# Pointwise convolution of a hybrid encoder block: from four plain column-block products to two groups of two blocks with seven-product pairs

## The chip, the cores and the metric

One Trainium2 chip, one of its cores. The metric is the device time of one execution in microseconds (us), the median of several runs. The program before takes 2043.55 us (three runs: 2043.1, 2043.55, 2046.21).

## The reference, cut to what matters

One layer of an encoder block works on x of 256 rows (two halves of 128) and 4096 columns. A projection by `w_in` gives q, k, v and z_a for a chunked attention, and a, g and z_c for a convolution module. The end of that module is what the change touches:

```python
u = jax.nn.silu(layer_norm(u, ln_g, ln_b))       # (256, 2048)
y_c = u @ w_pw + b_pw                            # w_pw: (2048, 2048)
y_c = rms_norm(y_c, conv_out_g) * jax.nn.silu(z_c)
h = h + concat([y_a, y_c]) @ w_out               # then a gated embedding, then a final norm
```

`u @ w_pw + b_pw` is the pointwise convolution: 256 rows by 2048 columns, a sum over 2048.

## The kernel before

**How a product is made.** Every fp32 operand is split into a high part (rounded to fp32r) and a low part (the rest), and a product is three matmuls: high by high, low by high, high by low. A matmul takes 128 of the sum's columns (a k-block), one half h of the rows, and 512 columns of the weight. For each weight tile `wt` of 128x1024 (512 KB, five buffers) ScalarE casts the high part `wh` (L203) and VectorE subtracts it to get the low part `wl` (L204); `wh` and `wl` have three buffers each, so the casts of a tile wait until TensorE has done with the tile three before it.

**Plain products.** `product` (L223) does one block of 512 columns in two of the four accumulator banks of PSUM, twelve matmuls for each weight tile.

**Seven-product pairs.** `mixed_product` (L324) does two column blocks j at once over both row halves h, in all four accumulator banks `c[h][j]`. Its k-blocks go in pairs, in an order written out as text; a pair is plain (eight products of three matmuls, 24) or, with a star, done by seven products (21 matmuls) in the manner of Strassen and Winograd. A starred pair needs more of the other engines: the two weight tiles are added up in four ways (`ua`, `ub`: L423, L424, L427, L428, VectorE, 128x512 each), and `ua` and `ub` are split like weights (`uh`, `ul`, two buffers each); three of the weight quarters are split as such, and one isn't. On the operand's side four sums of its quarters are needed, the combinations: `combine_again` (L275) rebuilds the quarters (L279, 128x512), forms four sums (L256 to L259, 128x128 each) and splits them (L264 ScalarE, L265 VectorE). Four of the seven products go into helper banks P1, P5, P6, P7, which are all four banks of the pool that the attention uses for its scores and transposes. After the last starred pair `on_helpers` runs: `helper_sums` (L461) adds the helpers up, four additions on VectorE that read PSUM. The end adds each accumulator to its sum, once for each quarter (h, j).

**The stage.** The attention's last heads come first (L829 to L858), then the pointwise convolution (L914 to L921): for each of four column blocks c a row of the bias is loaded and spread over the partitions, a plain `product` of 16 k-blocks runs on the operand `uS`, and VectorE adds the bias while reading PSUM (L919), and ScalarE takes the sum of squares (L497). Then come the combinations of all of x, `xS` (L926 to L930, eight times `combine_again`), and the products for z_a (`gated`, L932), two column blocks at a time by `mixed_product` in the order `delayed`: `1 3 5 7 0* 9 2* 11 4* 13 6* 15 8* 10 12 14`. `xS` lies first in that stage's needs when its fifth pair, `0*`, is reached.

**What sets the order.** The scheduler of the language lays the instructions of each engine into one fixed list when the program is built; at run time each engine takes its list in order and waits by semaphores. So VectorE's list holds, one after another, splits for weight tiles, combinations and additions, and whatever stands behind a waiting instruction waits too. SyncE's list holds the loads of weights and of bias rows in the same way. When the attention is done, its scratch pool is closed (L910) and a new pool takes its place (L911), in which the bias rows and the rows of the combinations share three buffers, and `ua` and `ub` share two.

Of the kernel before, what the change touches and what calls it, by code (L numbers as in the profile page):

```python
# [10 lines left out]
F32 = mybir.dt.float32  # L11
F32R = mybir.dt.float32r
AF = mybir.ActivationFunctionType
ALU = mybir.AluOpType
AX = mybir.AxisListType

P = 128
NB = 512
# [7 lines left out]
def hybrid_block(  # L26
# [23 lines left out]
    nc = tc.nc  # L50
    _, T, D = x.shape
    NH = T // P
    AW = attn_out_g.shape[1]
    CW = conv_out_g.shape[1]
# [6 lines left out]
    KCW = CW // P  # L61
# [10 lines left out]
    act = pool("act", 8)  # L72
# [8 lines left out]
    spool = pool("spool", 2, first_scratch, 1)  # L81
# [141 lines left out]
    def product(w, col, lhs, kblocks, pool=None, tag="acc", fills=2):  # L223

        acc = [
            (pool or ps_acc).tile([P, NB], F32, tag=tag, name=f"acc{h}") for h in range(NH)
        ]
        for k0 in range(0, kblocks, KC):
            kc = min(KC, kblocks - k0)
            wh, wl = weight_parts(w, col, k0, kc)  # L230
            for k in range(kc):
                for h in range(NH):
                    accumulate(acc[h], h, lhs, k0 + k, wh, wl, k, kblocks)
            fill(fills)
        return acc
# [10 lines left out]
    def sum_rows():  # L246
        return [spool.tile([P, NB], F32, tag="row", name="comb", bufs=3) for _ in range(2)]
# [27 lines left out]
    def combine_again(dst, at, t, i, rows, then=lambda ins: None):  # L275

        a, s = rows
        then(
            nc.vector.tensor_tensor(  # L279
                a.rearrange("q (i t) -> q i t", t=T), t[:, i : i + 2, 0, :].bitcast(F32),  # L280
                t[:, i : i + 2, 1, :].bitcast(F32), ALU.add,
            )
        )
        return combined_parts(dst, at, s, a[:, :T], a[:, T : T + P], a[:, T + P :], 1.0, then)
# [27 lines left out]
    def units(text):  # L312

        return [(int(u.rstrip("*")), u.endswith("*")) for u in text.split()]
# [4 lines left out]
    first = units("0 1 3 5 7 9 11 13 15 2* 8 4* 10 6* 12 14")  # L319
    early = units("1 3 5 7 0* 9 2* 11 4* 13 6* 15 8 10 12 14")  # L320
    final = units("1 0* 3 2* 5 4* 6* 7 8* 9 10* 12* 11 13 14 15")
    late = units("1 3 5 7 9 11 13 15 0* 2 4* 6 8* 10* 12 14")

    def mixed_product(  # L324
        w, col, lhs, comb, order, on_helpers, ahead=None, fills=(0,), on_begin=None, apart=NB,
# [9 lines left out]
        c = [[ps_acc.tile([P, NB], F32, tag="acc", name=f"acc{h}{j}") for j in range(2)] for h in range(NH)]  # L335
        helper = {}
# [55 lines left out]
        for n, (pair, seven) in enumerate(order):  # L392
            if n < done:
                continue
            if ahead:
                ahead(pair)
            wts = []
            for k in range(2):
                wt = wpool.tile([P, 2, NB], F32, tag="w", name="wt")
                nc.sync.dma_start(wt, two_columns(w, 2 * pair + k, col, apart))  # L400
                wts.append(wt)
            if n >= len(order) - n_left:
                for k in range(2):
                    tiles = left[2 * (n - len(order) + n_left) + k]
                    held.append((2 * pair + k, parts_of(wts[k], 2, tiles and tiles())[0]))
                fill(fills[n % len(fills)])
                continue
            if not seven:
                for k in range(2):
                    add_plain(n, k, *parts_of(wts[k], 2)[0])  # L410
                fill(fills[n % len(fills)])
                continue
            begins = not helper
            if begins:
                for name in ("P1", "P5", "P7", "P6"):
                    helper[name] = ps_tmp.tile([P, NB], F32, tag="tmp", name=f"acc_{name}")
                banks.update(helper)
            w0, w1 = wts
            ua = upool.tile([P, 2, NB], F32, tag="u", name="ua")
            ub = upool.tile([P, 2, NB], F32, tag="u", name="ub")  # L420
            plus = partial(nc.vector.tensor_tensor, op=ALU.add)
            w0h, w0l = parts_of(w0, 1)[0]
            plus(ua[:, 0], w0[:, 0], w0[:, 1])  # L423
            plus(ua[:, 1], w0[:, 1], w1[:, 1])  # L424
            uah, ual = pair_parts(ua)
            w1h, w1l = parts_of(w1, 2)[0]
            plus(ub[:, 0], ua[:, 0], w1[:, 1])  # L427
            plus(ub[:, 1], ub[:, 0], w1[:, 0])  # L428
            ubh, ubl = pair_parts(ub)
            first = len(made)  # L430

            def s_of(i):
                t, at = comb[pair // 4], pair % 4
                return [t[:, at + i // 2, q, (i % 2) * P : (i % 2 + 1) * P] for q in range(2)]

            k0, k1 = 2 * pair, 2 * pair + 1
            add("P1", block(k0, 0), (w0h[:, 0], w0l[:, 0]), n, True)
            add("P5", s_of(1), (uah[:, 0], ual[:, 0]), n, True)
            add("P7", s_of(0), (uah[:, 1], ual[:, 1]), n, True)
            add("P2", block(k1, 0), (w1h[:, 0], w1l[:, 0]), n, True)  # L440
            add("P3", s_of(3), (w1h[:, 1], w1l[:, 1]), n, True)
            add("P6", s_of(2), (ubh[:, 0], ubl[:, 0]), n, True)
            add("P4", block(k1, 1), (ubh[:, 1], ubl[:, 1]), n, True)
            if begins and on_begin:
                on_begin()
            if begins:
                tc.add_manual_dep(
                    made[first].ins, last_transpose[0].ins.name,
                    mybir.DependencyInfo(mybir.DependencyClass.NoSync, mybir.DependencyReason.DATA),
                    reason="transposes before the helpers take their banks",  # L450
                )
            if n == last_seven:
                on_helpers(helper)
            fill(fills[n % len(fills)])
# [3 lines left out]
    tt, stt = nc.vector.tensor_tensor, nc.vector.scalar_tensor_tensor  # L458
    QUARTERS = ((0, 0), (1, 0), (0, 1), (1, 1))

    def helper_sums(helper, z):  # L461


        nc.scalar.copy(z[1][0], helper["P1"])
        tt(z[1][0], helper["P6"], z[1][0], ALU.add)
        tt(z[0][1], helper["P5"], z[1][0], ALU.add)
        tt(z[1][0], helper["P7"], z[1][0], ALU.add)
        tt(z[1][1], helper["P5"], z[1][0], ALU.add)
# [26 lines left out]
    def square_sum(dst, src, scale=1.0):  # L495
        junk = spool.tile([P, NB], mybir.dt.bfloat16, tag="junk", name="junk", bufs=1)
        return nc.scalar.activation(junk[:, : src.shape[1]], src, AF.Square, scale=scale, accum_out=dst)  # L497
# [28 lines left out]
    def first_pairs(add):  # L526
# [62 lines left out]
        for n in range(1, n_x + 1):  # L589
# [26 lines left out]
    rows = [(conv_ln_g, KCW), (conv_ln_b, KCW), (b_dw, KCW), (attn_out_g, AW // P),  # L616
            (conv_out_g, KCW), (ple_norm_g, KD)]
    n_rows = sum(n for _, n in rows)
    at = [sum(n for _, n in rows[:i]) for i in range(len(rows))]
# [86 lines left out]
    uS = []  # L706
# [194 lines left out]
    def broadcast_row(src, n0, n):  # L901

        t = spool.tile([P, n], F32, tag="row", name="row", bufs=3)
        nc.sync.dma_start(
            t, bass.AP(tensor=src.tensor, offset=src.offset + n0, ap=[[0, P], [1, n]])
        )
        return t
# [3 lines left out]
    spool = upool = pool("lpool", 2, side=1)  # L911
    y_c = []
    ssq_c = cpool.tile([P, NH, CW // NB], F32, name="ssq_c")
    for c in range(CW // NB):  # L914
        row = broadcast_row(b_pw, c * NB, NB)
        acc = product(w_pw[0], c * NB, uS, KCW)
        y = act.tile([P, NH, NB], F32, tag="act", name="y_c")
        for h in range(NH):
            nc.vector.tensor_tensor(y[:, h, :], acc[h], row, ALU.add)  # L919
            square_sum(ssq_c[:, h, c : c + 1], y[:, h, :])  # L920
        y_c.append(y)  # L921
    nc.scalar.activation(idle_out, ssq_c[:, 0, 1:2], AF.Silu)
    r_c = rstd_of(ssq_c, CW, "r_c")

# [66 lines left out]
    for c0 in range(0, D // NB, 2):  # L991
        for j in range(2):
            hc = act.tile([P, NH, NB], F32, tag="act", name="hc")
            c = c0 + j
# [5 lines left out]
        def on_helpers(helper):  # L1000
            _, z = sum_tiles()
            h00, h01, h10, h11 = (hs[c0 + j][:, h, :] for h in range(NH) for j in range(2))
            tt(h00, helper["P1"], h00, ALU.add)
            helper_sums(helper, z)
            tt(h01, h01, z[0][1], ALU.subtract)
            tt(h10, h10, z[1][0], ALU.add)
            tt(h11, h11, z[1][1], ALU.subtract)

        acc = mixed_product(
            w_out[0], c0 * NB, yT, yS, dense if c0 else late, on_helpers,  # L1010
            ahead=y_ahead if c0 == 0 else before_last(h_ahead) if c0 + 2 == D // NB else None,
            fills=(2,),
        )
# [56 lines left out]
    c0 = n_f - 2  # L1070
    _, z = sum_tiles()
# [145 lines left out]
```

## Time and profile before

| | before |
|---|---|
| median of three runs | 2043.55 us |
| the profiled execution's own time | 2045.51 us |
| its span, first to last instruction | 2043.7 us |
| mean granted TensorE clock | 0.998 |
| busy: PE, DVE, ACT | 99%, 92%, 57% |
| loads of `w_pw` (32 of 512 KB), first and last issue | 889.9 and 981.0 us |
| additions of the bias (L919, 8), first and last start | 934.6 and 1000.9 us |

PE is TensorE's matmuls, PEld its weight loads, DVE is VectorE, ACT ScalarE, SP SyncE. "Busy" counts from an instruction's start to its modelled end; matmuls are pipelined, so the distance between the starts of neighbours tells their cost, and not their duration. In a timeline a row gives the start, the length, engine and line, what is written and read, the count, and in brackets how long the engine sat idle before it and what released it. All times below are from the start of the span.

### The profile page before, as it was taken

The page shows a single profiled execution, that of the slowest core. Times are in us where ns is not written, and L with a number is a line of the kernel's source. Part 1 is how long each engine was busy: PE and PEld are TensorE (multiplying, and loading weights), DVE is VectorE, ACT ScalarE, POOL GpSimd, SP SyncE. Part 2 cuts the span into 40 slices and gives each one's busy share as a digit, 9 for nine tenths or more (in the row PEclk, how much of TensorE's full clock was granted, in tenths as well). Part 3 has the DMA queues.
Part 4 walks back from the last instruction along what each step waited for, and adds up shares of the span by engine and source line. Part 5 has one row for each costly group of instructions (what it writes and reads, how often), then busy time and mean ns, then how long its engine had stood idle before and what let it go on. Part 6 is the DMA issues. An engine that isn't in the chain of part 4 may idle for free.

```text
span 2043.7 us, 25981 instructions
## 1 busy us (share of the span) xinstructions
PE 2025.3 (99%) x9127; PEld 1664.1 (81%) x9127; DVE 1870.3 (92%) x2657; ACT 1172.7 (57%) x1511; POOL 10.1 (0%) x19
## 2 busy tenths in 40 slices
PE   9999999999999999999999999999999999999997
PEld 7888888877888788888888888888888888888876
DVE  7999999899887998865889999999999999999998
ACT  7645535554564536565556656676565666655555
POOL 0000000000000000000000000000000000000000
PEclk9999999999999999999999999999999999999999
DMA  8666665656566665566666666676666656666765
GB/s 290 190 195 206 194 197 165 205 186 194 177 195 197 196 187 185 179 192 195 193 210 200 201 215 194 218 232 208 212 200 210 211 185 209 199 220 206 235 208 179
DMA packets 166236, 412.28 MB, mean 202 GB/s; under 512 B 13006, under 2 KB 16222, under 8 KB 166106
## 3 DMA queue, kind: packets, MB, share of 16 engines
q1 hardware_dynamic: 165456, 409.80, 63.6%
q8 instruction: 71, 1.16, 0.2%
q10 hardware_dynamic: 650, 0.84, 0.1%
q14 instruction: 59, 0.48, 0.1%
HBM read 406.39 MB, written 4.19 MB: 201 GB/s over the span
## 4 chain that ended last, share of the span: by engine, by line
PE 85%; DVE 9%; issue 3%; DMA 2%; ACT 1%; POOLq 0%; POOL 0%; ACTq 0%; DVEq 0%
PE acc L367 55%; PE acc L217 14%; PE acc_P L367 13%; DVE wl L204 4%; DVE cv L670 2%; DMA wt<-in_w_in_dram 1%; DVE ul L204 1%; PE tmp_ps L169 1%; DVE ub L428 0%; DVE ub L427 0%; DMA wt<-in_w_out_dram 0%; ACT wh L203 0%; PE tmp_ps L831 0%; DVE ua L423 0%; PE tmp_ps L849 0%
## 5 line engine op out<-in xcount | busy, mean ns | idle before, releaser
L367 PE MATMUL acc<-wh,big_t 128*128 128x512 f32 x3658 | 1131.0, 391 | 0.3 <-DVE z L943 0.3
L203 ACT CAST wh<-wt 128x1024 fp32r<-128x1024 f32 (+1 forms) x737 | 718.4, 984 | 599.4 <-PE acc L367 348.1
L204 DVE TENSOR_TENSOR wl<-wt,wh 128x1024 fp32r<-128x1024 f32 (+1 forms) x737 | 829.1, 1136 | 87.3 <-ACT wh L203 83.0
L367 PEld LDWEIGHTS acc<-wh,big_t 128*128 128x128 f32 x3658 | 684.4, 188 | 141.4 <-DVE z L943 0.7
L367 PE MATMUL acc<-wl,big_t 128*128 128x512 f32 x1829 | 704.5, 391 | 1.9 <-DVE wl L204 1.9
L367 PEld LDWEIGHTS acc<-wl,big_t 128*128 128x128 f32 x1829 | 342.7, 188 | 77.6 <-DVE wl L204 6.7
L217 PE MATMUL acc<-wh,big_t 128*128 128x512 f32 x816 | 254.1, 392 | 0.0
L670 DVE SCALAR_TENSOR_TENSOR cv<-uT,dw,cv 128x255 f32<-128x255 f32 (+25 forms) x480 | 203.5, 461 | 0.9
L203 ACT CAST uh<-ub 128x1024 fp32r<-128x1024 f32 x115 | 121.0, 1052 | 115.9 <-DVE ub L428 95.3
L367 PE MATMUL acc_P<-uh,big_t 128*128 128x512 f32 x588 | 179.6, 392 | 0.2
L217 PEld LDWEIGHTS acc<-wh,big_t 128*128 128x128 f32 x816 | 152.9, 188 | 31.2
L217 PE MATMUL acc<-wl,big_t 128*128 128x512 f32 x408 | 159.1, 390 | 0.0
L203 ACT CAST uh<-ua 128x1024 fp32r<-128x1024 f32 x115 | 121.1, 1053 | 63.7 <-DVE ua L424 58.7
L204 DVE TENSOR_TENSOR ul<-ub,uh 128x1024 fp32r<-128x1024 f32 x115 | 140.3, 1220 | 9.0 <-ACT uh L203 8.1
L204 DVE TENSOR_TENSOR ul<-ua,uh 128x1024 fp32r<-128x1024 f32 x115 | 140.2, 1219 | 0.8 <-ACT uh L203 0.3
L367 PEld LDWEIGHTS acc_P<-uh,big_t 128*128 128x128 f32 x588 | 109.1, 188 | 26.0 <-ACT uh L203 4.3
L367 PE MATMUL acc_P<-ul,big_t 128*128 128x512 f32 x294 | 112.7, 393 | 1.5 <-DVE ul L204 1.3
L423 DVE TENSOR_TENSOR ua<-wt 128x512 f32<-128x512 f32 x115 | 79.0, 687 | 22.7 <-DMA wt<-in_w_in_dram 17.7
L217 PEld LDWEIGHTS acc<-wl,big_t 128*128 128x128 f32 x408 | 76.6, 188 | 15.7
L424 DVE TENSOR_TENSOR ua<-wt 128x512 f32<-128x512 f32 x115 | 78.8, 685 | 3.6 <-DMA wt<-in_w_in_dram 2.9
L428 DVE TENSOR_TENSOR ub<-ub,wt 128x512 f32<-128x512 f32 x115 | 78.9, 686 | 1.0
L427 DVE TENSOR_TENSOR ub<-ua,wt 128x512 f32<-128x512 f32 x115 | 78.8, 685 | 0.2
(213 smaller groups left out, 1392.2 us busy)
## 6 DMA issues: line engine op xcount, KB each, us to landing
wt<-in_w_in_dram SPq DMA_DIRECT2D x447, 512.0 KB, 4.0
wt<-in_w_out_dram SPq DMA_DIRECT2D x128, 512.0 KB, 4.2
wt<-in_w_ple_gate_dram SPq DMA_DIRECT2D x128, 512.0 KB, 4.2
wt<-in_w_pw_dram SPq DMA_DIRECT2D x32, 512.0 KB, 4.4
hc<-in_x_dram SPq DMA_DIRECT2D x8, 512.0 KB, 5.5
wt<-in_w_ple_dram SPq DMA_DIRECT2D x8, 512.0 KB, 4.4
xin<-in_x_dram SPq DMA_DIRECT2D x7, 512.0 KB, 8.6
out_dram<-hc SPq DMA_DIRECT2D x12, 256.0 KB, 2.4
```

The source lines that it names most:

```text
L169: nc.tensor.transpose(pt[:, i * T + h * P : i * T + (h + 1) * P], src[:, h, b * P : (b + 1) * P], ident,)
L203: nc.scalar.copy(wh[:, :kc, :], wt[:, :kc, :]),
L204: nc.vector.tensor_tensor(wl[:, :kc, :], wt[:, :kc, :], wh[:, :kc, :].bitcast(F32), ALU.subtract),
L217: nc.tensor.matmul(acc, a, b[:, k, :], start=kb == 0 and kind == 0, stop=kb == kblocks - 1 and kind == 2,)
L367: nc.tensor.matmul(banks[name], a, b, start=name not in begun, stop=final and ends[name] == n and kind == 2 and not (left and name in "P2 ...
L423: plus(ua[:, 0], w0[:, 0], w0[:, 1])
L424: plus(ua[:, 1], w0[:, 1], w1[:, 1])
L427: plus(ub[:, 0], ua[:, 0], w1[:, 1])
L428: plus(ub[:, 1], ub[:, 0], w1[:, 0])
L670: nc.vector.scalar_tensor_tensor(cv[:, i, PAD - k :], uT[:, i, : T + k - PAD], dw[:, b, k : k + 1], cv[:, i, PAD - k :], ALU.mult, ALU.add,)
```

## The change

The pointwise convolution goes through `mixed_product` in two groups of two column blocks. The first group takes its eight pairs of k-blocks in the order `1 3 5 0* 4 2* 6 7`, the second in the order `1 0* 3 2* 5 4* 6 7`. The combinations of the operand for pairs 0 and 2 are made ahead of the first group, those for pair 4 between the groups; they are found by pair in a dictionary. The bias is no longer added while the accumulators are read: it is added to (or, for j = 1, subtracted from) the helpers' sums in SBUF, and the accumulators are added to these at the end.

```diff
+    point = [units("1 3 5 0* 4 2* 6 7"), units("1 0* 3 2* 5 4* 6 7")]
...
-                t, at = comb[pair // 4], pair % 4
+                t, at = comb[pair] if isinstance(comb, dict) else (comb[pair // 4], pair % 4)
...
-    for c in range(CW // NB):
-        row = broadcast_row(b_pw, c * NB, NB)
-        acc = product(w_pw[0], c * NB, uS, KCW)
-        y = act.tile([P, NH, NB], F32, tag="act", name="y_c")
-        for h in range(NH):
-            nc.vector.tensor_tensor(y[:, h, :], acc[h], row, ALU.add)
-            square_sum(ssq_c[:, h, c : c + 1], y[:, h, :])
-        y_c.append(y)
+    uC = {}
+
+    def point_combinations(pair, t, at):
+        combine_again(t, at, uS[pair // 2], 0, sum_rows())()
+        uC[pair] = (t, at)
+
+    t = spool.tile([P, 4, 2, T], F32R, tag="comb", name="comb_t", bufs=1)
+    for c in range(2):
+        point_combinations(2 * c, t, 2 * c)
+
+    def point_pair(c0, order):
+
+        ys = [act.tile([P, NH, NB], F32, tag="act", name="y_c") for _ in range(2)]
+        z = [[y[:, h, :] for y in ys] for h in range(NH)]
+
+        def on_helpers(helper):
+            rows = [broadcast_row(b_pw, (c0 + j) * NB, NB) for j in range(2)]
+            nc.scalar.copy(z[0][0], helper["P1"])
+            helper_sums(helper, z)
+            for h, j in QUARTERS:
+                tt(z[h][j], z[h][j], rows[j], ALU.subtract if j else ALU.add)
+
+        acc = mixed_product(w_pw[0], c0 * NB, uS, uC, order, on_helpers)
+        for h, j in QUARTERS:
+            tt(z[h][j], acc[h][j], z[h][j], ALU.subtract if j else ALU.add)
+            square_sum(ssq_c[:, h, c0 + j : c0 + j + 1], z[h][j])
+        y_c.extend(ys)
+
+    point_pair(0, point[0])
+    point_combinations(4, spool.tile([P, 2, 2, T], F32R, tag="stage", name="comb_p"), 0)
+    point_pair(2, point[1])
```

The lines of the changed file stand one lower than before from L322 on, and 24 lower behind the stage.

## The prediction

> **What bounds the kernel now.** I read first the page's shares of busy time and its chain, then the chain in order of time, then windows around the stage, then the timelines of single engines.
>
> ```profile
> PE 2025.3 (99%) x9127; PEld 1664.1 (81%) x9127; DVE 1870.3 (92%) x2657; ACT 1172.7 (57%) x1511; POOL 10.1 (0%) x19
> ...
> PE 85%; DVE 9%; issue 3%; DMA 2%; ACT 1%; POOLq 0%; POOL 0%; ACTq 0%; DVEq 0%
> ```
>
> TensorE bounds the whole, VectorE comes close behind. The chain in order of time shows the stage itself:
>
> ```profile
> 928.18 72.36 PE acc L217 x319
> 1000.54 21.76 PE acc L367 x96
> ```
>
> From the attention's end to the start of z_a the chain is matmuls without a break, and 21.76 / 96 = 0.2267 us is what one costs. So a matmul less is worth 0.2267 us here, as long as nothing else comes to bound the stage. How much room has VectorE? The windows (columns: PE, PEld, DVE, ACT, POOL busy, granted clock, DMA) from the end of the attention to the second sum `ub` of z_a's first starred pair, and after it:
>
> ```profile
> 930.24:1019.89 89.65, 89.65 (x398) 74.21 (x397) 65.36 (x98) 46.85 (x61) 3.70 (x2) 1.00 0.66 203
> 1019.89:1063.00 43.11, 43.11 (x192) 35.70 (x191) 37.83 (x42) 24.58 (x27) 0.00 (x0) 1.00 0.64 206
> ```
>
> VectorE is busy for 65.36 of 89.65 us, so it has 24.3 us to spare; behind that it is at 88%, with little to give back.
>
> **What the change takes away.** A starred pair has 21 matmuls for 24. Two stars in the first group and three in the second take away 15 matmuls, 15 x 0.2267 = 3.4 us. Loads are as many as before, 32 of weights and 4 of the bias.
>
> **What it puts on VectorE.** The distances between starts give the pace of work that stands ready:
>
> ```profile
> 1014.32 0.29 DVE L259 SCALAR_TENSOR_TENSOR comb<-comb 128x128 f32<-128x128 f32 x1
> 1014.52 0.69 DVE L424 TENSOR_TENSOR ua<-wt 128x512 f32<-128x512 f32 x1
> 1015.12 0.69 DVE L427 TENSOR_TENSOR ub<-ua,wt 128x512 f32<-128x512 f32 x1
> 1015.72 1.22 DVE L204 TENSOR_TENSOR wl<-wt,wh 128x1024 fp32r<-128x1024 f32 x1
> 1016.86 0.69 DVE L265 TENSOR_TENSOR comb_t<-comb,comb_t 128x512 fp32r<-128x512 f32 x1
> ...
> 1019.20 0.69 DVE L428 TENSOR_TENSOR ub<-ub,wt 128x512 f32<-128x512 f32 x1
> ```
>
> 128x128 goes by in about 0.205 us, 128x512 in 0.60, 128x1024 in 1.135. VectorE's list between the reduction for `r_a` (L501) and that second `ub` of z_a's pair 0* holds before: 33 of 128x1024, 29 of 128x512, 32 of 128x128, 4 tiny (0.07), 61.7 us at this pace. In the changed list the same stretch holds 40, 74, 43 and 4: 45.4 + 44.4 + 8.8 + 0.3 = 98.9 us. The 37.2 us more are five starred pairs (four sums, two big splits and a half one each, in place of two big splits), three combinations, and for each group four additions of the helpers and four of the bias beside the four final ones. VectorE had 24.3 us to spare, so it now becomes the bound of this stretch.
>
> **The sum, from both engines' lists.** The stretch starts for TensorE with the last matmul of the attention, for VectorE with the reduction for `r_a`, which waits for ScalarE's squares of `y_a`:
>
> ```profile
> 927.79 0.39 PE L856 MATMUL tmp_ps<-v,pT 128*128 128x128 f32 x2
> 927.93 0.48 PE L217 MATMUL acc<-wl,big_t 128*128 128x512 f32 x1
> ```
>
> ```profile
> 930.02 0.19 ACT L497 ACTIVATION_READ_ACCUMULATOR junk<-y_a 128x1 f32 x1
> 930.12 1.03 ACT L203 CAST wh<-wt 128x1024 fp32r<-128x1024 f32 x1
> ```
>
> ```profile
> 930.24 0.16 DVE L501 TENSOR_REDUCE r_a<-ssq_a 128x2 f32<-128x8 f32 x1 [1.94 <-ACT junk L497]
> ```
>
> Up to there both programs issue the same attention work between as many matmuls, so I take these times over. In the changed list 423 matmuls follow before the P6 of z_a's 0*, which needs the cast of that `ub`. Without a wait TensorE would be there at 928.0 + 423 x 0.2267 = 1023.9. VectorE gets its `ub` done at 930.24 + 98.9 = 1029.1, plus its own waits. I followed the three lists pair by pair with these durations and found seven of its waits, 2.2 us in all, the longest 0.7 for the cast of `ua` in the second group's 0*. By bounds: no waits, or about 4 us if each of the six starred pairs had that longest one. So 1031.3, and the cast takes 1.05:
>
> ```profile
> L203 ACT CAST uh<-ua 128x1024 fp32r<-128x1024 f32 x115 | 121.1, 1053 | 63.7 <-DVE ua L424 58.7
> ```
>
> TensorE comes to it at 1032.4, having idled 8.5 us. The next pair, 2*, costs once more: 27 matmuls on TensorE (6.1 us, 1038.5), while VectorE's list has about 6 us up to its `ua`, and the cast of that stands behind one of `wh` that needs a buffer; I put 1.3 us there, between 0 and 2. Then `delayed` has plain pairs again and VectorE catches up. Idle 8.5 + 1.3 = 9.8, less 3.4 saved: **6.4 us slower**.
>
> **Where the idle falls.** The largest piece is the entry to 0* of the first group. TensorE has 17 matmuls ready behind the attention and is through at 931.9. The P5 product needs the cast of `ua` and the high part of the first combination. VectorE's list has, behind `r_a`, the two combinations interleaved with the sums: three of 128x512 for the rebuilt quarters and the second half of `ua`, one more for its first half, and three small ones; `ua` is done at about 933.7. The cast brings 934.7, the cast of the combination (0.62 in the row below) 935.3. That is a wait of 3.4 us in one piece, and 0.6 more for the low parts, since `ul` (1.22) and L265 (0.69) still follow: 4.0 us. Some 1.5 us fall in the second group (its first casts and its first `uh`), the rest in z_a.
>
> ```profile
> L264 ACT CAST big_t<-comb 128x512 fp32r<-128x512 f32 x6 | 3.7, 617 | 1.0 <-DVE comb L259 1.0
> ```
>
> **Edits that I cost at nothing.** The first group needs all four accumulator banks while two still hold v. These are read here, and the second read ends at 907.87:
>
> ```profile
> 905.66 0.69 ACT L886 ACTIVATE v<-acc,r_x 128x512 f32<-128x512 f32 x1 [1.21 <-PE acc L217]
> ...
> 907.18 0.69 ACT L886 ACTIVATE v<-acc,r_x 128x512 f32<-128x512 f32 x1
> ```
>
> The scores end near 906.6, six matmuls go to the two free banks first, the third bank is asked for at 908.0 and the fourth at 908.7: hidden; without that cover it would be under 1.3 us. Between the groups the four banks come free by four additions of 0.6, while TensorE's list ends each bank's sum three matmuls (0.68) after the one before: 0 to 0.3 us, inside the term of 1.5. The bias rows share buffers with the combinations' rows, so their loads, and two weight loads behind the first of them on SyncE, wait until about 937; loads of `w_pw` land in 4.4 us (row below), and ScalarE asks for the first of these weights near 944: hidden by some 2 us. ScalarE gets some 11 us more (starred pairs' casts, combinations, copies of P1) in a window with 42.8 to spare; where it is late it is for VectorE, as above.
>
> ```profile
> wt<-in_w_pw_dram SPq DMA_DIRECT2D x32, 512.0 KB, 4.4
> ```
>
> **The rivals.**
>
> *TensorE's clock drops at the entry.* The wait there is in one piece. The kernel's first matmuls show a slow TensorE:
>
> ```profile
> 1.18 2.31 PE L124 MATMUL tmp_ps<-idle 128*128 128x512 bf16 x5 [1.18 <-DVE ssq_f L1025]
> ...
> 7.65 1.17 PE L367 MATMUL acc<-wh,big_t 128*128 128x512 f32 x4
> ```
>
> Five take 2.31 with a last one of 0.63, so 0.42 us apart against 0.2267, and some 6 us later the four are 0.26 apart. If 3.4 us of waiting bring that state back for as long, 15 matmuls cost 0.19 more each, 2.9 us: 9.3 us slower in all, 2052.9; half as long would make 7.8. Against it: whether 3.4 us are enough no row of before tells, since its matmuls never pause so long behind the start.
> The Trainium skill (TensorE: Matmul & The Clock Gate, "Why this matters for your kernels") says to have no idle gap above about 3 us between bursts of matmuls, since one idle window brings half the clock back; by its window of 3.4 us at half pace I estimate 1.7 us more. The slow start agrees, 0.42 against 0.2267 us; the granted clock in the profile's rows doesn't show that start.
>
> *Only the entry costs.* If VectorE catches up inside the groups, 4.0 - 3.4 = 0.6 slower, 2044.2. For it: in the window of before it waits 18 times for ScalarE's `wh`, which waits for buffers, so it isn't at its limit there. Against it: 37.2 us into 24.3. It would need about 8.5 - 4.0 = 4.5 us less work on its list than I count.
>
> ```profile
> DVE wl L204 <- ACT wh L203: 23.7, 18, 2.1
> ```
>
> *The other side: the work hides, 15 matmuls gone, 3.4 us faster, 2040.2.* It decides at the entry: the combinations only need `uS`, split long before (889). Were they ahead of `r_a` in time, the P5 would find its operands. Against it: in VectorE's list they stand behind `r_a`, which can't start before 930.24, and TensorE is at the P5 at 931.9; about 6 us of work can't be done in 1.7.
>
> *VectorE waits longer:* with 4 us of waits in place of 2.2 and 2 us at z_a's 2*, 8.9 slower, 2052.5.
>
> **How the numbers follow.** The sum against the profiled execution is 2045.51 + 6.4 = 2051.9 (span 2043.7 + 6.4 = 2050.1); that execution was 2.0 us above the median of the runs, so for medians I forecast 2043.55 + 6.4 = **2049.9 us**. Chances: this case, with its bounds from 4.2 to 8.2 us slower, 0.58; the clock 0.12; longer waits 0.05; only the entry 0.18; hidden 0.07. The range goes from the entry alone, 2044.2, to the clock's 2052.9: it leaves out the hidden case and little more. Some 0.2% (4.1 us) is what a measurement of this kernel can tell from no change. Within it lie the last two cases, 0.18 + 0.07 = 0.25; faster by more gets 0.01, as no case here gains over 3.4; slower by more 0.58 + 0.12 + 0.05, less that 0.01, = 0.74.
>
> **What would show it.** In the profile after: 15 matmuls fewer on `mixed_product`'s and `product`'s lines together; TensorE idle for about 3.4 us near 932, released by ScalarE's cast of `ua` or of the combination, in front of P5; VectorE at 95% or more from 930 to 1030; TensorE waiting again at z_a's 0* for the cast of `ub`; its idle time in the stretch near 9.8 us. I am wrong if VectorE shows gaps in the two groups, if TensorE runs through at 932, or if matmuls behind 935 are spaced by more than 0.23 us.

## The result and the profile after

The changed kernel takes 2051.63 us (median of 8 runs, 2050.26 to 2052.51), the kernel before 2044.74 us beside it (8 runs): ratio 1.0032, 95% interval 1.0021 to 1.0043, so 6.9 us slower; 6.4 was forecast. (Of the distance from the forecast median, 2049.9, 1.2 us is the kernel before itself: 2043.55 over three runs, 2044.74 over eight.) The profiled execution of the changed kernel took 2050.94 us (span 2049.2). Its page, shares of busy time and chain:

```profile
PE 2025.3 (99%) x9112; PEld 1662.3 (81%) x9112; DVE 1902.8 (93%) x2721; ACT 1183.3 (58%) x1528; POOL 21.0 (1%) x19
...
PE 85%; DVE 10%; issue 3%; DMA 1%; ACT 1%; SPq 0%; POOLq 0%; POOL 0%; ACTq 0%; DVEq 0%
```

TensorE has 15 matmuls fewer and the same busy time: what was saved came back as slower matmuls and waits. The same two windows as before (PE, PEld, DVE, ACT, POOL busy, granted clock, DMA share, GB/s):

```profile
930.24:1019.89 89.65, 86.74 (x371) 70.29 (x372) 88.27 (x134) 52.10 (x71) 12.56 (x1) 0.98 0.66 210
1019.89:1063.00 43.11, 40.81 (x170) 32.23 (x169) 41.33 (x59) 24.21 (x28) 1.02 (x1) 0.96 0.58 178
```

VectorE went from 65.36 of 89.65 us to 88.27 (98%), and TensorE is no longer busy throughout. TensorE's timeline shows where it stops, at the first group's 0* and at z_a's 0*:

```profile
928.90 1.20 PE L368 MATMUL acc<-wh,big_t 128*128 128x512 f32 x4
932.97 1.19 PE L368 MATMUL acc_P<-uh,comb_t 128*128 128x512 f32 x2 [2.87 <-issue]
...
1027.74 0.63 PE L368 MATMUL acc_P<-wh,big_t 128*128 128x512 f32 x2
1030.67 0.73 PE L368 MATMUL acc_P<-uh,big_t 128*128 128x512 f32 x2 [2.30 <-ACT uh L203]
```

Four matmuls from 928.90 are through by 929.81 (4 x 0.2267), so the first pause is 3.16 us; two from 1027.74 are through by 1028.19, so the second is 2.48. The granted clock in 3 us windows behind both:

```profile
933.00:936.00 3.00, 3.00 (x7) 2.22 (x8) 3.00 (x6) 0.95 (x2) 0.00 (x0) 0.50 0.44 151
936.00:939.00 3.00, 3.00 (x14) 2.41 (x14) 3.00 (x4) 1.23 (x3) 0.00 (x0) 0.94 0.85 182
...
1030.00:1033.00 3.00, 2.33 (x8) 1.92 (x9) 3.00 (x4) 1.14 (x2) 0.00 (x0) 0.82 0.76 212
1033.00:1036.00 3.00, 3.00 (x9) 2.33 (x9) 2.71 (x5) 1.24 (x2) 0.00 (x0) 0.61 0.68 193
1036.00:1039.00 3.00, 3.00 (x15) 2.44 (x14) 2.92 (x4) 2.77 (x3) 0.00 (x0) 1.00 0.87 283
```

Twice, then, some 3.4 us went by at half clock, 7 to 9 matmuls in 3 us for 13.2: about 1.7 us of TensorE's pace each time. How much of that the kernel loses is another question (runs 5, 6 and 10). The Trainium skill (TensorE: Matmul & The Clock Gate, "Why this matters for your kernels") warns of pauses above about 3 us; the first agrees, the second is shorter.

**One measure for all runs.** The place of the stage drifts by some 3 us from profile to profile, in code that all share. So I measure the *stretch* from the last attention matmul to z_a's first eviction (L943 before, L967 after), cut in two at z_a's P6, the matmul that waits for `uh` of `ub`. Windows with these bounds, before, a repeat of it, after, and a repeat of that:

```profile
927.79:1082.70 154.91, 154.91 (x687) 128.28 (x686) 117.77 (x157) 83.69 (x103) 3.70 (x2) 1.00 0.64 201
```

```profile
927.38:1082.30 154.92, 154.92 (x687) 128.24 (x686) 117.84 (x156) 83.59 (x103) 3.69 (x2) 1.00 0.64 201
```

```profile
925.49:1030.67 105.18, 99.78 (x428) 79.63 (x426) 101.88 (x164) 62.84 (x88) 14.65 (x2) 0.98 0.58 186
1030.67:1088.27 57.60, 57.60 (x245) 46.96 (x246) 50.25 (x57) 30.74 (x33) 0.00 (x0) 0.97 0.67 210
```

```profile
927.53:1033.33 105.80, 100.06 (x428) 79.67 (x426) 101.88 (x164) 62.65 (x88) 14.65 (x2) 0.98 0.57 184
1033.33:1089.39 56.06, 56.06 (x245) 45.83 (x246) 50.02 (x57) 30.74 (x33) 0.00 (x0) 1.00 0.71 216
```

The stretch is 154.91 and 154.92 before, 162.78 and 161.86 after: 7.9 and 6.9 us lost. Behind it nothing changed: 2043.7 - 1082.70 = 961.0, 2049.2 - 1088.27 = 960.9.

### The profile page after: what moved, and what is told of

It is laid out like the page before. It is cut to its first block, busy times and chain, and to the rows that moved or that the text cites. A ratio compares the mean times of both kernels' runs of the same rounds, so it can differ in the third digit from the quotient of the medians.

```text
span 2049.2 us, 26032 instructions
## 1 busy us (share of the span) xinstructions
PE 2025.3 (99%) x9112; PEld 1662.3 (81%) x9112; DVE 1902.8 (93%) x2721; ACT 1183.3 (58%) x1528; POOL 21.0 (1%) x19
## 4 chain that ended last, share of the span: by engine, by line
PE 85%; DVE 10%; issue 3%; DMA 1%; ACT 1%; SPq 0%; POOLq 0%; POOL 0%; ACTq 0%; DVEq 0%
PE acc L368 58%; PE acc_P L368 14%; PE acc L217 9%; DVE wl L204 3%; DVE cv L671 2%; DMA wt<-in_w_in_dram 1%; DVE ul L204 1%; PE tmp_ps L169 1%; ACT wh L203 0%; DVE ub L429 0%; PE tmp_ps L832 0%; PE tmp_ps L850 0%; PE tmp_ps L817 0%; DVE ub L428 0%; ACT uh L203 0%
## 5 line engine op out<-in xcount | busy, mean ns | idle before, releaser
L368 PE MATMUL acc<-wh,big_t 128*128 128x512 f32 x3844 | 1188.8, 392 | 2.9 <-DVE z L967 1.4
L368 PEld LDWEIGHTS acc<-wh,big_t 128*128 128x128 f32 x3844 | 719.4, 188 | 151.7 <-ACT big_t L155 2.1
L368 PE MATMUL acc<-wl,big_t 128*128 128x512 f32 x1922 | 738.7, 391 | 0.8 <-DVE wl L204 0.6
L368 PEld LDWEIGHTS acc<-wl,big_t 128*128 128x128 f32 x1922 | 360.5, 188 | 78.8 <-DVE wl L204 4.2
L203 ACT CAST uh<-ub 128x1024 fp32r<-128x1024 f32 x120 | 126.2, 1051 | 113.6 <-DVE ub L429 94.7
L217 PE MATMUL acc<-wh,big_t 128*128 128x512 f32 x560 | 173.3, 390 | 0.0
L203 ACT CAST uh<-ua 128x1024 fp32r<-128x1024 f32 x120 | 126.4, 1053 | 65.1 <-DVE ua L425 60.4
L204 DVE TENSOR_TENSOR ul<-ub,uh 128x1024 fp32r<-128x1024 f32 x120 | 146.3, 1219 | 7.8 <-ACT uh L203 6.7
L204 DVE TENSOR_TENSOR ul<-ua,uh 128x1024 fp32r<-128x1024 f32 x120 | 146.2, 1219 | 0.2
L217 PEld LDWEIGHTS acc<-wh,big_t 128*128 128x128 f32 x560 | 105.0, 188 | 21.5
L217 PE MATMUL acc<-wl,big_t 128*128 128x512 f32 x280 | 109.0, 389 | 0.0
L424 DVE TENSOR_TENSOR ua<-wt 128x512 f32<-128x512 f32 x120 | 82.3, 686 | 19.4 <-DMA wt<-in_w_in_dram 14.1
L425 DVE TENSOR_TENSOR ua<-wt 128x512 f32<-128x512 f32 x120 | 82.1, 684 | 4.1 <-DMA wt<-in_w_in_dram 2.9
L368 PE MATMUL acc<-uh,big_t 128*128 128x512 f32 x240 | 74.4, 390 | 0.0
```

Source lines behind the costliest of these rows:

```text
L203: nc.scalar.copy(wh[:, :kc, :], wt[:, :kc, :]),
L204: nc.vector.tensor_tensor(wl[:, :kc, :], wt[:, :kc, :], wh[:, :kc, :].bitcast(F32), ALU.subtract),
L217: nc.tensor.matmul(acc, a, b[:, k, :], start=kb == 0 and kind == 0, stop=kb == kblocks - 1 and kind == 2,)
L368: nc.tensor.matmul(banks[name], a, b, start=name not in begun, stop=final and ends[name] == n and kind == 2 and not (left and name in "P2 ...
```

## The experiments

Theory A is the prediction's: VectorE works off one list in order, and its length from the attention to z_a's first starred pair sets the time. Theory B: the pauses cost through the half clock. Theory C: VectorE has no spare time that can be moved, so that each starred pair, or each hole in VectorE's work, costs by itself.

In the table, "from v" starts at ScalarE's first read of v (L886 before, at 905.66) in place of the last attention matmul. It holds also where a kernel draws matmuls into the attention (runs 4, 8 and 12 have 7 fewer in the stretch, 665 recorded for 672, or 1.6 us). Before it is 1082.70 - 905.66 = 177.04, after 1088.27 - 903.40 = 184.87:

```profile
903.40 0.69 ACT L887 ACTIVATE v<-acc,r_x 128x512 f32<-128x512 f32 x1 [1.21 <-PE acc L217]
```

| run | median against before (95%) | stretch, of it to P6 | from v, against before |
|---|---|---|---|
| before | | 154.91 | 177.04 |
| after | 1.0032 (1.0021-1.0043) | 162.78, 105.18 | +7.83 |
| 1 `r_a` later | 1.0041 (1.0026-1.0057) | 161.30, 105.33 | +6.38 |
| 2 no bias additions | 1.0019 (1.0010-1.0029) | 157.55 | +2.63 |
| 3 second group only | 1.0015 (1.0006-1.0025) | 157.82, 101.60 | +2.91 |
| 4 combinations ahead | 1.0009 (0.9999-1.0018) | 154.72, 98.51 | +1.48 |
| 5 busy entry | 1.0030 (1.0021-1.0039) | 161.86, 104.36 | +6.93 |
| 6 busy z_a | 1.0033 (1.0021-1.0045) | 161.98, 106.04 | +7.03 |
| 7 z_a's order | 1.0024 (1.0014-1.0033) | 160.93 | +6.00 |
| 8 ahead, and order | 1.0004 (0.9995-1.0013) | 153.70 | +0.45 |
| 9 before again | one time, 2044.31 us | 154.92 | +0.01 |
| 10 after again | one time, 2052.04 us | 161.86, 105.80 | +6.95 |
| 11 before, VectorE loaded | 1.0016 (1.0007-1.0025) | 158.91 | +4.01 |
| 12 ahead, no bias additions | 1.0001 (0.9992-1.0010) | 152.35 | -0.83 |

### 1. `r_a` behind the first group

```diff
-    r_a = rstd_of(ssq_a, AW, "r_a")
...
     point_pair(0, point[0])
+    r_a = rstd_of(ssq_a, AW, "r_a")
```

> Only the place of r_a's sum is changed: it stands behind the first group instead of ahead of it, so that VectorE takes the combinations of pair 0 and the first low parts without waiting for ScalarE's last square sum. In the changed kernel VectorE is idle for 1.93 us ahead of r_a's sum. Theory A (VectorE's in-order list from the end of the attention to z_a's first seven-product unit sets the time): the 1.93 us of idle time go, the entry wait of 3.16 us falls to about 1.2 to 1.6, and the stretch from the last attention matmul to z_a's first eviction goes from 162.78 to about 161 (160.5 to 161.5). Theory B (what is lost are the two stretches at half clock, about 1.7 us each, with the waits that bring them): the entry pause becomes too short to bring the half clock, and 1.7 us more go beside the 1.9: about 159 to 159.5. Theory C (the list does not matter, the waits are made elsewhere): no change, 162.5 to 163.

VectorE's first combination now stands where `r_a` stood, and VectorE's timeline shows it waiting just as long:

```profile
927.30 0.69 DVE L279 TENSOR_TENSOR comb<-big_t 128x512 f32<-128x512 f32 x1 [1.94 <-ACT junk L498]
```

So `r_a` was not the gate. The scratch pool is renewed at this point, and the combination's rows may take the place of the attention's scratch, `junk` among it; that is read from the code, no run shows it. To P6 it stays at 105.33. The stretch is shorter by 1.48 all the same, all of it behind P6:

```profile
1030.19:1086.16 55.97, 55.97 (x245) 45.79 (x246) 50.03 (x57) 30.71 (x33) 0.00 (x0) 1.00 0.71 216
```

The clock stayed at 1.00 behind the pause at z_a, in 55.97 us for 57.60. The 161 that I expected came out for another reason than mine.

### 2. Without the bias additions

```diff
         helper_sums(helper, z)
-        for h, j in QUARTERS:
-            tt(z[h][j], z[h][j], rows[j], ALU.subtract if j else ALU.add)
```

> The eight additions of the convolution's bias to the helpers' sums are left out (the bias is not added, the rows are still loaded): 8 x about 0.6 = 4.8 us of VectorE less, four in each group, nothing else. Theory A (VectorE's list sets the time): the stretch from the last attention matmul to z_a's first eviction goes from 162.78 to about 158 (157.5 to 158.8); the wait at z_a's first seven-product unit is gone or nearly so, and with it maybe the half clock there, which would give up to 1.7 more (156.3). Theory B (the two half clocks are what is lost; VectorE only in that it starts them): the entry is as it was, with its half clock; at most the second one goes: 161 or more.

```profile
926.76:1084.31 157.55, 154.65 (x672) 125.52 (x671) 147.23 (x213) 93.71 (x120) 2.32 (x2) 0.99 0.63 201
```

VectorE has 4.9 us less (152.13 to 147.23), the stretch 5.23; the wait at z_a is gone, the half clock with it. The entry is as before, half clock and all. Theory A's number; B's, 161 or more, is excluded. (Against run 10, the changed kernel without a second fall, 161.86, the gain is 4.3 us for the 4.9.)

### 3. Starred pairs in the second group only

```diff
-    point_pair(0, point[0])
+    for c in range(2):
+        row = broadcast_row(b_pw, c * NB, NB)
+        acc = product(w_pw[0], c * NB, uS, KCW)
...
     point_pair(2, point[1])
```

> The first two column blocks are made by the old plain product with the bias at the eviction; only the second two go by three pairs of seven products. 9 matmuls fewer than before (9 x 0.2267 = 2.0 us). VectorE's list to z_a's first seven-product unit is some 12 to 14 us shorter than in the changed kernel. Theory A: that is below what VectorE had to spare, no wait of over 0.5 us at z_a's first unit, so the stretch from the last attention matmul to z_a's first eviction is about 153 (152.5 to 154) against 154.9 before and 162.8 after, and the kernel is faster than before by about 1 to 2 us (ratio 0.9990 to 0.9998). Theory C (a seven-product unit in this stage costs by itself, whatever VectorE has to spare: its loss is per unit, 7.9/5 = 1.6 each on top of the 0.7 saved): 157.5 to 158.

157.82, theory C's number; A's sum failed by 4.8 us. VectorE's and TensorE's timelines between the groups:

```profile
943.60 1.22 DVE L204 TENSOR_TENSOR wl<-wt,wh 128x1024 fp32r<-128x1024 f32 x1 [0.38 <-ACT wh L203]
949.06 0.69 DVE L424 TENSOR_TENSOR ua<-wt 128x512 f32<-128x512 f32 x1 [4.23 <-DMA wt<-in_w_pw_dram]
...
956.20 1.28 DVE L948 TENSOR_TENSOR y_c<-acc,row 128x512 f32<-128x512 f32 x2
```

```profile
956.95 0.73 PE L368 MATMUL acc<-wh,big_t 128*128 128x512 f32 x2 [1.97 <-DVE y_c L948]
```

VectorE stands idle for 4.23 us, waiting for the weights of the first starred pair. Then that pair's sums stand in its list ahead of the second block's additions of the bias (956.20), for whose banks the group waits: TensorE loses 2 us. From 957.00 on VectorE is busy for 64.92 of 68.99 us and is late again at z_a (two waits of 0.5 and 0.6):

```profile
957.00:1025.99 68.99, 67.91 (x296) 55.26 (x297) 64.92 (x106) 41.96 (x56) 6.28 (x1) 1.00 0.60 184
```

What VectorE does not use in the first two blocks is lost, since it cannot work on weights that are not there yet. The three waits named make 3.05 us of the 4.9 by which the stretch lies above 154.91 - 2.0; the rest is in pieces that leave no gap on TensorE's timeline.

### 4. Combinations made ahead

```diff
-    for c in range(2):
-        point_combinations(2 * c, t, 2 * c)
...
+        later.extend(partial(combination_ahead, pair) for pair in (0, 2))
```

`later` is the queue of small work that `mixed_product` and `product` draw from (`fills`); the combinations get tiles of their own there.

> The combinations of pairs 0 and 2 of the first group are made ahead, among the attention's queued work, in tiles of their own, and not at the entry. VectorE's list behind the attention is shorter by the two combinations: about 2 x (0.6 + 4 x 0.2 + 0.6) = 4 us; the attention stage has them instead, where VectorE has room. Theory A: the entry wait falls from 3.16 us to under 1, without the half clock behind it, and the stretch from the last attention matmul to z_a's first eviction from 162.78 to about 158.5 (158 to 159.5). Theory B (half clocks): the first one goes with its pause, -1.7 and -3.2, less what later waits take back: 158 to 159 too, but with the wait at z_a's first unit unchanged (2.5) and not larger.

```profile
927.53:1026.04 98.51, 96.47 (x420) 77.32 (x418) 95.76 (x149) 61.09 (x85) 10.09 (x2) 1.00 0.61 198
1026.04:1082.25 56.21, 56.21 (x245) 45.73 (x246) 51.22 (x59) 30.48 (x33) 0.00 (x0) 1.00 0.70 215
```

The stretch fell to 154.72, further than the 158.5 of A. Part of that is bookkeeping: 7 matmuls (1.6 us) moved ahead of its start. From v the gain over the changed kernel is 6.35: VectorE has 6.1 us less to P6 (101.88 to 95.76), and the clock stays up throughout. Two waits are left, at the entry and at z_a, and the kernel is still 1.5 us behind before:

```profile
936.94 0.72 PE L368 MATMUL acc_P<-uh,comb_a 128*128 128x512 f32 x2 [0.50 <-ACT uh L203]
...
1026.04 0.74 PE L368 MATMUL acc_P<-uh,big_t 128*128 128x512 f32 x2 [1.50 <-ACT uh L203]
```

### 5 and 6. TensorE kept busy in the pauses

```diff
+            def busy_matmuls(count):
+                for _ in range(count if begins else 0):
+                    nc.tensor.matmul(helper["P6"], block(k0, 0)[0], w0h[:, 0], start=True, stop=True)
+
+            busy_matmuls(busy[0])
             add("P5", s_of(1), (uah[:, 0], ual[:, 0]), n, True)
...
+            busy_matmuls(busy[1])
             add("P6", s_of(2), (ubh[:, 0], ubl[:, 0]), n, True)
```

`busy` is (13, 0) for the first group in the one, (0, 10) for z_a's in the other.

> 13 extra matmuls (13 x 0.2267 = 2.95 us) into the helper bank P6, which is begun afresh afterwards, stand where TensorE waited 3.16 us at the first group's first seven-product unit; nothing is left out. They keep TensorE busy so that its clock should not fall there (8 matmuls took 3.5 us at half clock, 1.7 more than at full). Theory A (VectorE's list sets when z_a's unit can go on, so that what the entry loses is absorbed): from the last attention matmul to the matmul of P6 in z_a's first unit it stays at 105.2 (104.8 to 105.6), only the wait there grows from 2.5 to about 4. Theory B (half clocks cost by themselves): that time falls by 1.7 to about 103.5 and the wait at z_a's unit stays at 2.5.

The clock stayed at 1.00 behind the entry:

```profile
925.29:1029.65 104.36, 101.27 (x440) 80.97 (x439) 101.66 (x164) 62.65 (x88) 14.64 (x2) 1.00 0.58 187
1029.65:1087.15 57.50, 57.50 (x245) 46.97 (x246) 50.20 (x58) 30.60 (x33) 0.00 (x0) 0.97 0.67 210
```

```profile
1029.65 1.22 PE L368 MATMUL acc_P<-uh,big_t 128*128 128x512 f32 x2 [2.30 <-ACT uh L203]
```

104.36 lies between A's 105.2 and B's 103.5, and the wait at z_a is as long as in the changed kernel, 2.30 in the profile, where A had about 4. The matmul of P4 that reads `ul`, the last of the first starred pair, in the changed kernel, in run 5 and in the changed kernel's repeat (run 10):

```profile
938.99 0.39 PE L368 MATMUL acc<-ul,big_t 128*128 128x512 f32 x1
```

```profile
937.93 0.39 PE L368 MATMUL acc<-ul,big_t 128*128 128x512 f32 x1
```

```profile
941.66 0.39 PE L368 MATMUL acc<-ul,big_t 128*128 128x512 f32 x1
```

From the last attention matmul that is 13.50, 12.64 and 14.13 us. So the half clock at the entry cost 0.86 us in the first profile and 1.49 in the repeat, and not 1.7. The difference is in front of the low part of the first combination, for which TensorE waits in any case:

```profile
934.08 0.50 PE L368 MATMUL acc_P<-uh,comb_t 128*128 128x512 f32 x1 [0.37 <-DVE comb_t L265]
```

```profile
936.30 0.50 PE L368 MATMUL acc_P<-uh,comb_t 128*128 128x512 f32 x1 [0.36 <-DVE comb_t L265]
```

These rows are run 5 and the repeat; in the first profile the same matmul starts at 934.39. From the last attention matmul it is 8.79, 8.77 and 8.90 us, so nearly the same with and without a fall. In the first profile the clock is down from 933 on, and the slow matmuls up to there run under this wait; in the repeat it falls behind it (1.00 from 933 to 936, 0.50 from 937 to 940).

What the entry lost then reached P6 whole: 105.18 - 104.36 = 0.82 for 0.86, 105.80 - 104.36 = 1.44 for 1.49, and in runs 1 and 6, with 13.66 and 14.13 at the same matmul, 0.97 for 1.02 and 1.68 for 1.49. So A is wrong in that a loss at the entry is absorbed; B is right in that it adds to the rest, and had its size too large.

How the loss gets into VectorE's list, the changed kernel's VectorE shows; these two gaps are missing in run 5:

```profile
946.54 1.23 DVE L204 TENSOR_TENSOR ul<-ub,uh 128x1024 fp32r<-128x1024 f32 x1 [0.24 <-ACT uh L203]
...
956.42 2.73 DVE L939 TENSOR_TENSOR y_c<-acc,y_c 128x512 f32<-128x512 f32 x4 [0.32 <-PE acc L368]
```

The same four additions start at 955.39 in run 5. From `r_a` on (927.94 and 927.74) that is 28.48 and 27.65 us, 0.83 apart. A late TensorE gives its buffers and banks back late, and VectorE waits for them.

> 10 extra matmuls (10 x 0.2267 = 2.27 us) into the helper bank P6 before it is begun, where TensorE waited 2.47 us at z_a's first seven-product unit; nothing is left out. Theory A as corrected by the first runs (VectorE's list up to that unit; behind it TensorE sets the time again, and the half clock there costs its 1.7 in full): up to P6 the stretch stays at 105.2 (104.8 to 105.6), behind it 57.6 becomes about 56.0, so 161.2 in all for 162.78. If the 2.2 us lost behind P6 are waits for later units and not the clock: 57.6 stays.

```profile
1032.78:1088.72 55.94, 55.94 (x245) 45.79 (x246) 49.90 (x58) 30.63 (x33) 0.00 (x0) 1.00 0.67 216
```

Behind P6 55.94 for 57.60, as expected, 1.66 us: there, where TensorE sets the time again, the half clock costs in full. Since the clock stayed up in runs 1 and 10 too, where the pause was not filled, this run does not show that filling it was the reason. To P6 it was 106.04, 0.4 above A's bound, with an entry that lost 1.49.

### 7 and 8. z_a's starred pairs later

```diff
-    delayed = units("1 3 5 7 0* 9 2* 11 4* 13 6* 15 8* 10 12 14")
+    delayed = units("1 3 5 7 9 11 13 0* 15 2* 4* 6* 8* 10 12 14")
```

> Only z_a's order is changed: its first seven-product unit stands behind seven plain pairs in place of four (1 3 5 7 9 11 13 0* 15 2* 4* 6* 8* 10 12 14). A plain pair is 24 matmuls, 5.4 us of TensorE, and 2 low parts, 2.3 us of VectorE, so each one ahead gives VectorE 3.1 us to catch up: 9.3 us for the 9.1 lost. Theory A (a list that is late by a fixed amount): no wait at z_a's first unit, no half clock; what is left lost is the entry, 3.2 and 1.7 at half clock and small waits of about 1: the stretch to z_a's first eviction is 154.9 - 3.4 + 5.9 = 157.4 (156 to 158.5). Theory C (VectorE is bound for the whole of z_a's group too, so that order only moves the wait): 161 or more, the waits at the seven-product units that now follow each other.

160.93: A's 157.4 fell, C holds. The single wait at z_a is gone, but where the starred pairs now follow each other VectorE is at its limit, 21.04 of 22 us:

```profile
1040.00:1062.00 22.00, 22.00 (x97) 17.54 (x96) 21.04 (x25) 13.00 (x16) 0.00 (x0) 1.00 0.62 203
```

Over the whole stretch VectorE has 151.91 us of work, and TensorE, with 15 matmuls fewer, 154.91 - 3.4 = 151.5. With so much on both, an order has little room to hide a wait in; two were tried. Beside the combinations made ahead, with `1 3 5 7 9 0* 11 2* 13 4* 15 6* 8* 10 12 14`:

> The combinations made ahead, as in the run on that (stretch 154.72, of it 0.5 of a wait at the entry and 1.5 in one piece at z_a's first unit), and beside it z_a's first seven-product unit behind five plain pairs in place of four, which gives VectorE 5.4 - 2.3 = 3.1 us. Theory A: the wait at z_a's first unit is gone, the stretch is about 152.5 to 153.3 against 154.9 before, and the kernel about 1 to 2 us faster than before if the rest is as long (ratio 0.9990 to 0.9997). Theory C: the waits move on to the later units, and the stretch stays at 154.5 or above.

The wait at z_a fell from 1.50 to 0.64, the stretch to 153.70, between A's and C's numbers, again with 7 matmuls drawn ahead: from v it is 0.45 us longer than before, and the medians cannot be told apart (0.9995 to 1.0013). Not the gain expected.

### 9 and 10. Both kernels again

> The kernel before once more, for how far a profile repeats: the stretch from the last attention matmul to z_a's first eviction was 154.91. If the stretch is a sound measure it comes out within 0.5 of that, whatever the start of the stretch does (it lay between 924.4 and 927.8 in the runs so far, behind code that is the same in all).

> The changed kernel once more: 162.78 with two falls of the clock, one at the entry and one at z_a's first unit. In the run with r_a moved the second fall stayed away though the pause was as long, and 1.66 with it. If that was the move's doing the stretch is again 162.8; if the second fall is a matter of the moment, it is 161.1 or 162.8 with a wait of about 2.5 in both cases.

The stretch of before repeats within 0.01 us. In the changed kernel's repeat TensorE paused at z_a as in the first profile, and the clock did not fall:

```profile
1033.33 0.73 PE L368 MATMUL acc_P<-uh,big_t 128*128 128x512 f32 x2 [2.30 <-ACT uh L203]
```

```profile
1033.00:1036.00 3.00, 2.67 (x12) 2.22 (x13) 3.00 (x4) 0.80 (x2) 0.00 (x0) 1.00 0.79 218
1036.00:1039.00 3.00, 3.00 (x15) 2.43 (x14) 3.00 (x5) 2.76 (x3) 0.00 (x0) 1.00 0.79 253
```

So the second fall is a matter of the moment, and run 1's gain was luck. Without it the change costs 6.9 us.

### 11. Before, with VectorE loaded

```diff
             nc.vector.tensor_tensor(y[:, h, :], acc[h], row, ALU.add)
+            for _ in range(2):
+                tt(y[:, h, :], y[:, h, :], row, ALU.subtract)
+                tt(y[:, h, :], y[:, h, :], row, ALU.add)
```

> The kernel before with four more additions on each of the 8 column halves of the pointwise stage (the bias row taken off and added again, twice): 32 x 0.6 = 19.2 us of VectorE, spread over the four blocks, TensorE's work unchanged; nothing is left out. My ledger gave VectorE 24.3 us to spare in that stage. Theory A (the sum of the whole stage counts): all of it fits, the stretch stays at 154.9 to 155.5. Theory C (time that VectorE does not use in the first blocks cannot be used later, because what it would work on is not there yet; only what is left at z_a's first unit counts, where the cast was done at 1021.4 and the matmul came at 1026.2): the 9.6 us in the first two blocks are free, of the 9.6 in the last two about 5 are, and the rest, 4 to 5, is lost: 159 to 160.

```profile
926.78:1085.69 158.91, 156.73 (x687) 127.65 (x686) 135.69 (x189) 82.65 (x103) 5.04 (x2) 1.00 0.62 196
```

VectorE got 17.9 us more by its busy time and 4.0 were lost, near C's 4 to 5; A is excluded. The matmul that the expectation puts at 1026.2 starts earlier in the kernel before, so that C's own count would have been 9.6 - 4.1 = 5.5:

```profile
1025.53 0.61 PE L367 MATMUL acc_P<-uh,big_t 128*128 128x512 f32 x2
```

Nor are the losses quite where C had them: TensorE's timeline names three waits of 0.39, one in each of the first three blocks, and one of 0.95 at 1009.78, where z_a begins, all for `wl`.

### 12. Both lightenings

The edits of 2 and 4 together.

> Two of the lightenings together: the combinations of pairs 0 and 2 made ahead, and the eight bias additions left out (the bias is not added). Apart they took 8.06 and 5.23 us off the stretch of 162.78. Theory A (TensorE sets the time as soon as VectorE's list is short enough, and then the 15 matmuls show): no wait over 0.5 at z_a's first unit, clock at full, the stretch is 154.91 - 3.4 and up to 0.7 of small waits: 151.5 to 152.2, and the kernel 0.1 to 0.2% faster than before. Theory C (VectorE bound everywhere, every hole counts): 154.72 - 4.8 would be 149.9, which TensorE's own matmuls do not allow; waits of over 1 in all stay, 152.5 to 153.5.

```profile
929.47:1081.82 152.35, 151.35 (x665) 123.43 (x664) 142.46 (x200) 92.40 (x118) 8.35 (x2) 1.00 0.65 207
```

152.35 looks like A, but with the 7 matmuls drawn ahead it is 154.0; from v the gain over before is 0.83 of the 3.4 saved, and the median shows none (0.9992 to 1.0010). Waits of 0.50 at the entry and 0.51 at z_a are on TensorE's timeline; the other 1.6 us are in pieces too short for it. The waits of its weight loads, these two among them, name what TensorE waits for, 1.8 us in five waits and 1.5 in three:

```profile
PEld acc_P L368 <- DVE ul L204: 1.8, 5, 0.9
PEld acc_P L368 <- ACT uh L203: 1.5, 3, 0.9
```

Behind the stretch the kernels with the combinations ahead also take longer, 962.6, 963.1 and 961.6 us to the end of the span in runs 4, 8 and 12 for 961.0 and 960.2 in the two profiles of before; why, no run shows. So from v flatters them a little. Even 9.7 us less on VectorE (152.13 to 142.46) do not free the 15 matmuls' time; how much more would, was not tried. No version here is measurably faster than the kernel before.

## Why the forecast held, and where it did not

- **TensorE's saving.** 15 matmuls went, as said. Their 3.4 us never came out whole; run 12 saw 0.83 of them.
- **VectorE's list becomes the bound.** Right. From `r_a` (927.94) to P6 (1030.67) it took 102.73 us, and 1029.65 - 927.74 = 101.91 in run 5, without the half clock at the entry; forecast were 98.9 of work, 2.2 of waits and 1.05 of a cast, 102.2. VectorE is at 98%, and taking work off the list moves the time (runs 2 and 4).
- **Idle 8.5 us at z_a's 0\*.** Right as lateness. In run 5 TensorE would have been at P6 without a wait at 925.50 + 423 x 0.2267 = 1021.4; it came at 1029.65, 8.3 late. With the half clock at the entry it is 925.70 + 423 x 0.2267 = 1021.6 and 1030.67, 9.1 late, and 9.7 in the repeat. As idle time it did not come: the forecast's sign was 9.8 us in the stretch, and the windows show 99.78 + 57.60 of 162.78 us busy, which leaves 5.4 without a matmul (5.7 in the repeat). The rest is slow matmuls, and waits that the modelled ends cover.
- **1.3 us at z_a's 2\*.** After has 423 matmuls ahead of P6; with the same number still to come, 15 further on in its list, before needs 1082.70 - (928.0 + 438 x 0.2267) = 55.4 to the first eviction. After took 57.6 in the first profile and 56.06 in the repeat: 2.2 and 0.65. So the waits there were mis-sized, 0.65 for 1.3, and in the first profile the half clock added 1.5. Sum: 9.1 + 2.2 - 3.4 = 7.9, and 9.7 + 0.65 - 3.4 = 6.95, as measured.
- **Entry of 3.4 us in one piece.** 3.16, in front of P5, with 0.39 for the low part, forecast as 0.6. The profile names no releaser there ("issue"), but the cast of the combination ends at 932.87, 0.1 us before the matmul:

```profile
932.26 0.61 ACT L264 CAST comb_t<-comb 128x512 fp32r<-128x512 f32 x1
```

- **Edits that were costed at nothing.** The profile shows no cost. During the attention (900 to 926) TensorE's weight loads wait as they did before, 1.1 us for `s` and 0.6 for `pT`, and for no bank; between the groups TensorE has no gap; no wait of VectorE or ScalarE from 926 to 1031 is put down to a load. In the second group (940 to 1020) the weight loads wait 1.7 us in all, for the 1.5 forecast.
- **The clock as a rival.** It did fall, at the entry in every profile that kept the pause (after, 1, 2, 6, 7, 10), and with it came a sign that the prediction had named as one of being wrong: behind 935 matmuls start 0.43 us apart (935.28, 935.71, 936.13). The rival's term was 1.4 to 2.9 us on top of 6.4. By run 5 the fall is worth 0.8 at P6 in the first profile and 1.4 in the repeat. Without any fall the sum would be 8.3 + 0.65 - 3.4 = 5.5; with the entry's fall it is the repeat's 6.95. So the forecast, which left the clock out, lies so near to 6.9 in part by luck: 1.4 us that it left out stand against 0.9 of idle and of waits that it had too large. The clock can also fall at z_a, where I had not looked, and there it costs 1.5 to 1.7, nearly all of it.
- **Only the entry costs; the work hides.** Neither came. Run 4 has the hidden case's condition, the combinations ahead of `r_a`, and still lost 1.5 from v in place of winning 3.4: the combinations were not the only thing late.
- **The step that was wrong without showing: 24.3 us to spare.** In run 11, 19.2 us put into that room cost 4.0; in run 3 half the change cost 2.9. Work can only be laid into a gap when its data is there, and in an in-order list it holds up what stands behind it. The full change was sized right because its list left VectorE hardly a gap from `r_a` to P6 (the profile names waits of 1.1 us in all), so that its sum was nearly its length; for half the change the same reasoning missed by 4.8 us.

## What to carry to other kernels

Trading matmuls for sums on another engine pays only while that engine has room at the place where the sums stand in its queue; a share of busy time over the stage does not say that, as 19 us into 24 cost 4 here. Add up the in-order list between the two places where the bounding engine must meet it: if it leaves no gap, its sum is the time; if it leaves gaps, see what each gap waits for. A list without gaps does not absorb what the other engine loses on the way: it waits for that engine's banks and buffers, and the half clock at the entry came out whole at the end. Where the list is the bound, take instructions off it or make them earlier, where there is room, before touching the pauses that it makes.

## What the runs showed of the hardware

A pause of 2.5 us was followed by half clock in two profiles (after, 5) and not in two others (1, 10), with the same instructions around it; the pause of 3 us at the entry was followed by it each time, in six profiles, and with that pause filled by matmuls (run 5) the clock stayed up. Each fall lasted some 3.4 us. At z_a it cost 1.5 to 1.7 us, at the entry 0.9 to 1.5, where part of it could lie under a wait that was there anyway. The Trainium skill (TensorE: Matmul & The Clock Gate, "What's actually happening") describes a window of 3.4 us that runs freely, not in step with the program; that the same pause has either outcome agrees, but by its table an idle window is needed, and neither 2.5 nor 3.16 us can fill one.
